# Attention scores as plain float32 products of two heads on the two halves of the array's rows

## The chip, the core and the metric

The kernel runs on one NeuronCore of a Trainium2 chip. Its engines work side by side and meet only at semaphores: TensorE (PE in the profile; its weight loads are PEld), VectorE (DVE), ScalarE (ACT), GpSimd (POOL) and SyncE (SP), which issues most of the DMAs. On-chip memory is SBUF; TensorE writes into PSUM. The metric is the device time of one execution in microseconds (us), lower is better. The times given are medians of several executions; the profile is one further execution with its own time.

## What is computed

One layer of an encoder: a windowed attention with grouped queries (256 tokens, 2048 features, 32 query heads, 8 key heads of 64 features, four query heads for each key head), then a squared-ReLU MLP, each with a modulation by a condition vector before it and a LayerNorm behind it. The change touches the attention between the rotary positions and the values:

```python
def windowed_gqa_sink(h, positions, w_qkv, b_qkv, sink, w_o, b_o):
    proj = h @ w_qkv + b_qkv
    q, k, v = jnp.split(proj, [...], axis=-1)
    q = q.reshape(B, S, ATTN_KV_HEADS, ATTN_GROUP, ATTN_HEAD_DIM)
    k = k.reshape(B, S, ATTN_KV_HEADS, ATTN_HEAD_DIM)
    ...
    q = apply_rope(q, ...); k = apply_rope(k, ...)
    ...
    s = jnp.einsum('bnqhgd,bnkhd->bnhgqk', qb, kw).astype(jnp.float32) * (ATTN_HEAD_DIM ** -0.5)
    s = jnp.where(valid[None, :, None, None], s, -jnp.inf)
    m = jnp.maximum(jnp.max(s, axis=-1, keepdims=True), sk)
    p = jnp.exp(s - m)
    p = p / (jnp.sum(p, axis=-1, keepdims=True) + jnp.exp(sk - m))
    o = jnp.einsum('bnhgqk,bnkhd->bnqhgd', p.astype(vw.dtype), vw)
    return o.reshape(B, S, ATTN_Q_HEADS * ATTN_HEAD_DIM) @ w_o + b_o
```

## The kernel before

All data is float32. The large products (query-key-value projection, output projection, both MLP layers) are made of three products in the float32r format: each operand is split into a high part in float32r and the rest, and `mm3` (L499 to L502) adds high by high, high by low and low by high into one PSUM bank. A weight arrives as 1 MB in a `raw` buffer (SP issues it at L204); ACT makes the high part `wh` (L249), DVE the low part `wl` (L220).

The attention is laid over the projections. After the queries, keys and first values are there, 21 slots run (L866): in a slot the weights of one projection step are multiplied in two parts of 12 matmuls each (L500 to L502, 128x512), first those of the last value columns (`qkv`, slots 0 to 4), then those of the output projection (`project`). Around and between the parts stand the pieces of the attention: `scores(n)` ahead of slot n, `normalise(n)` and `probs_T(n-1)` in its middle, `values(n-1)` behind every second slot, and the rotation and transposition of the next block of queries. n counts 16 units; a unit is four query heads for 128 query tokens. j is the block of eight query heads (two key heads), `t` the half of the tokens.

- `split_k` and `split_q` (L661 to L678): after the rotation (`rope`), ACT writes the float32r high part of keys or queries and DVE the low part. For queries the two parts of a head stand side by side (64 + 64 columns); for keys each part stands twice.
- `heads_T` (L680): TensorE transposes blocks of 128x128 (L687, in float32r, against `identr`), eight for a call, and ACT copies them out of PSUM (L689). A transposed block of queries has the 64 high features on the upper rows and the 64 low ones on the lower rows. Keys take four calls, each block of queries two.
- `scores(n)` (L705): for each of four heads of one key head, two float32r matmuls over all 128 rows, 256 keys wide (L718 with the keys' high part, L719 with their low part). DVE adds the mask and takes the minimum (L724), ACT the exponential (L733).
- `normalise` (L738): ACT scales the probabilities (L748).
- `probs_T` (L751): eight float32 transposes (L758), two ACT copies (L760).
- `values(n)` (L763): four float32 matmuls of 512 columns into 64 PSUM rows each, two on the lower and two on the upper half of the array's columns (L773); ACT and DVE split the result (L775, L776).

Two further pieces are in the same stage. The modulation rows (`Mod`) multiply streamed weights with the condition vector: `quad` (L309) puts four float32 matmuls on four strips of 32 array columns. Behind the last projection step stand the sums of the LayerNorm: `add_gated` (L781 to L783), `norm_scalars` (L787 to L797), `normed` (L812 on DVE, L810 on ACT), and then the transposes of the MLP's input (L936).

What order the instructions have on an engine is decided by the scheduler of the framework when the kernel is built; each engine then runs its own list in that order. So a change in one place can move others.

Of the kernel before, what the change touches and what calls it, by code (L numbers as in the profile page):

```python
# [11 lines left out]
F32 = mybir.dt.float32  # L12
# [7 lines left out]
D = 2048  # L20
# [28 lines left out]
def hybrid_kernel(ctx: ExitStack, tc: tile.TileContext, a, out: bass.AP):  # L49
# [39 lines left out]
    identr = cst.tile([128, 128], F32R, name="identr")  # L89
    nc.vector.tensor_copy(identr, ident)  # L90
# [570 lines left out]
    def split_k(A):  # L661
        hl = [[g4(F32R) for _ in range(2)] for _ in range(NT)]
        for t in range(NT):
            s = A[:, t * 512:t * 512 + 512].rearrange("p (h d) -> p h d", h=8)
            vh, vl = (z.rearrange("p (h e d) -> p h e d", h=8, e=2) for z in hl[t])
            for e in range(2):
                nc.scalar.copy(vh[:, :, e], s)
                nc.vector.tensor_sub(vl[:, :, e], s, f32(vh[:, :, e]))
        return hl

    def split_q(A):
        hl = [g4(F32R), g4(F32R)]
        for t in range(NT):
            v = hl[t].rearrange("p (h x d) -> p h x d", h=8, x=2)
            s = A[:, t * 512:t * 512 + 512].rearrange("p (h d) -> p h d", h=8)
            nc.scalar.copy(v[:, :, 0], s)
            nc.vector.tensor_sub(v[:, :, 1], s, f32(v[:, :, 0]))
        return hl  # L678

    def heads_T(src):  # L680

        out = g4(F32R)
        for pr in range(2):
            pt = pst.tile([128, 512], F32R, name="pt")
            for i in range(2):
                for t in range(NT):
                    nc.tensor.transpose(pt[:, i * 256 + t * 128:i * 256 + t * 128 + 128],  # L687
                                        src(t, pr * 2 + i), identr)
            nc.scalar.copy(out[:, pr * 512:pr * 512 + 512], f32(pt))  # L689
        return out  # L690

    kT = {}

    def k_heads(khl, half):
        for x in range(2):
            o = heads_T(lambda t, i: khl[t][x][:, (half * 4 + i) * 128:(half * 4 + i) * 128 + 128])
            for q in range(4):
                kT[x, half * 4 + q] = o[:, q * 256:q * 256 + 256]

    def q_heads(qhl, half):  # L700
        return heads_T(lambda t, i: qhl[t][:, (half * 4 + i) * 128:(half * 4 + i) * 128 + 128])

    qA, qhl, qT, PS, PP, PT, oT = {}, {}, {}, {}, {}, {}, {}

    def scores(n):  # L705

        j, s, t = n // 4, n % 2, n % 4 // 2
        g = 2 * j + s
        hs = slice(4 * g, 4 * g + 4)
        pss = []  # L710
        nm = sml.tile([128, 4], F32, name="nm")
        for rp in range(2):
            ps = psa.tile([128, 512], F32, name="pa")
            for i in range(2):
                r = 2 * rp + i
                o = ps[:, i * 256:i * 256 + 256]
                lq = qT[j, s][:, r * 256 + t * 128:r * 256 + t * 128 + 128]
                nc.tensor.matmul(o, lq, kT[0, g], start=True, stop=False)  # L718
                nc.tensor.matmul(o, lq, kT[1, g], start=False, stop=True)  # L719

            pv = ps.rearrange("p (i k) -> p i k", i=2)
            for i in range(2):
                h = 4 * g + 2 * rp + i
                nc.vector.tensor_tensor_reduce(out=pv[:, i], in0=pv[:, i], in1=msk[:, t], scale=-1.0,  # L724
                                               scalar=nsnk[:, h:h + 1], op0=OP.add, op1=OP.min,
                                               accum_out=nm[:, 2 * rp + i:2 * rp + i + 1])
            pss.append(pv)
# [476 lines left out]
```

## Time and profile before

| | us |
|---|---|
| median of three runs | 1105.11 (1102.15 to 1106.28) |
| profiled execution, its own time | 1102.22 |
| its span (first to last instruction) | 1100.4 |
| PE busy | 1071.0 |
| DVE busy | 810.7 |
| ACT busy | 535.0 |
| granted TensorE clock, mean | 0.995 of full speed |

The span has a loading stage (until about 156 us), the attention slots with the projections (156 to about 360 us), the first LayerNorm, and the MLP (from 369 us to the end). In the rows of the timeline the columns are: start in us, busy time in us, engine, line, operation, what it writes from what, array rows and columns and moving shape, and how many records were merged. Matmuls are pipelined, so a single one shows a longer time (0.28 or 0.39 us) than the distance between two starts (0.12 or 0.23 us); what a piece costs is read from starts. A plain float32 matmul leaves two records in the trace, a float32r one and a transpose leave one.

### The profile page before, as it was taken

How to read it: one execution, taken by the hardware profiler on the slowest of the kernel's cores; microseconds unless marked ns; L12 is line 12 of the kernel's file. 1: busy time of each engine (PE TensorE's matmuls, PEld its weight loads, DVE VectorE, ACT ScalarE, POOL GpSimd, SP SyncE). 2: the span in 40 equal slices, each digit the busy share in tenths (PEclk: the TensorE clock that was granted, in tenths of full speed). 3: DMA queues.
4: the chain of work that ended last, by engine and by line, in shares of the span. 5: the costliest groups of instructions: out<-in, count | busy, mean ns of one | idle time of the engine just before them, and what ended most of it. 6: DMA issues, size and time to landing. Idle time of an engine off the chain costs nothing.

```text
span 1100.4 us, 15640 instructions
## 1 busy us (share of the span) xinstructions
PE 1071.0 (97%) x6154; PEld 870.8 (79%) x6154; DVE 810.7 (74%) x1175; ACT 535.0 (49%) x832; POOL 30.0 (3%) x54
## 2 busy tenths in 40 slices
PE   8889999999999899999999999999999999999995
PEld 6667677767677799988888888888888888888884
DVE  5597899979899787764588889756666556665676
ACT  5332448876772736643345443344553334544340
POOL 1000000001000000000000010001000000000001
PEclk9999999999999999999999999999999999999998
DMA  9999986679985896555578778766555555557521
GB/s 384 425 426 426 426 364 258 245 279 377 416 325 205 345 357 255 192 191 191 191 279 310 278 290 334 304 231 211 186 189 191 197 198 187 178 187 267 192 76 76
DMA packets 43337, 292.70 MB, mean 266 GB/s; under 512 B 5104, under 2 KB 5232, under 8 KB 9472
## 3 DMA queue, kind: packets, MB, share of 16 engines
q1 hardware_dynamic: 39312, 279.85, 66.4%
q0 software_dynamic: 3200, 10.50, 2.8%
q10 hardware_dynamic: 752, 1.35, 0.3%
q8 instruction: 48, 0.79, 0.3%
q14 instruction: 25, 0.20, 0.0%
HBM read 289.57 MB, written 2.11 MB: 265 GB/s over the span
## 4 chain that ended last, share of the span: by engine, by line
PE 88%; DMA 6%; DVE 4%; ACT 1%; issue 1%; SPq 0%; DVEq 0%; ACTq 0%
PE pa L1030 16%; PE pa L500 16%; PE pa L502 16%; PE pa L501 16%; PE pa L1031 8%; DMA raw<-in_modm 3%; PE pa L1007 3%; PE pa L1006 3%; PE pa L1008 3%; PE pm L309 3%; DMA raw<-in_wqkv 3%; PE pa L773 2%; PE pt L758 1%; DVE wl L220 1%; PE pa L718 1%; PE pt L687 1%
## 5 line engine op out<-in xcount | busy, mean ns | idle before, releaser
L220 DVE TENSOR_TENSOR wl<-raw,wh 128x1024 fp32r<-128x1024 f32 x332 | 403.4, 1222 | 218.8 <-ACT wh L249 218.1
L249 ACT CAST wh<-raw 128x1024 fp32r<-128x1024 f32 x332 | 347.2, 1053 | 441.7 <-PE pa L502 221.8
L500 PE MATMUL pa<-wh,g 128*128 128x512 f32 x816 | 322.2, 396 | 6.4 <-ACT g L521 3.1
L502 PE MATMUL pa<-wh,g 128*128 128x512 f32 x816 | 318.1, 392 | 2.1 <-DVE g L523 2.1
L501 PE MATMUL pa<-wl,g 128*128 128x512 f32 x816 | 319.4, 391 | 0.0
L1030 PE MATMUL pa<-g,wh 128*128 128x512 f32 x768 | 270.1, 397 | 0.0
L1031 PE MATMUL pa<-g,wl 128*128 128x256 f32 x768 | 214.8, 280 | 0.0
L500 PEld LDWEIGHTS pa<-wh,g 128*128 128x128 f32 x816 | 153.4, 188 | 44.4 <-ACT g L521 4.2
L502 PEld LDWEIGHTS pa<-wh,g 128*128 128x128 f32 x816 | 153.1, 188 | 39.2 <-DVE g L523 5.3
L501 PEld LDWEIGHTS pa<-wl,g 128*128 128x128 f32 x816 | 153.5, 188 | 32.4 <-issue 1.7
L1030 PEld LDWEIGHTS pa<-g,wh 128*128 128x128 f32 x768 | 144.2, 188 | 36.0 <-issue 0.8
L1031 PEld LDWEIGHTS pa<-g,wl 128*128 128x128 f32 x768 | 144.8, 189 | 0.1
L347 DVE SCALAR_TENSOR_TENSOR g<-raw,cact,g 128x1024 f32<-128x1024 f32 x65 | 82.8, 1280 | 1.1 <-DMA raw<-in_modf 0.6
L1007 PE MATMUL pa<-g,wh 128*128 128x256 f32 x256 | 72.5, 284 | 0.6 <-DVE g L950 0.5
L1006 PE MATMUL pa<-g,wh 128*128 128x256 f32 x256 | 72.6, 286 | 0.3 <-ACT g L942 0.3
L1008 PE MATMUL pa<-g,wl 128*128 128x256 f32 x256 | 72.3, 283 | 0.0
L309 PE MATMUL pm<-raw,cact 128*32 128x256 f32 (+2 forms) x776 | 48.4, 370 | 3.3 <-DMA raw<-in_modm 3.0
L1006 PEld LDWEIGHTS pa<-g,wh 128*128 128x128 f32 x256 | 48.8, 192 | 1.4 <-issue 0.8
L1007 PEld LDWEIGHTS pa<-g,wh 128*128 128x128 f32 x256 | 49.0, 192 | 1.0 <-DVE g L950 1.0
L1008 PEld LDWEIGHTS pa<-g,wl 128*128 128x128 f32 x256 | 49.1, 192 | 0.0
L347 DVE SCALAR_TENSOR_TENSOR g4b<-raw,cact,g4b 128x1024 f32<-128x1024 f32 x32 | 40.7, 1280 | 10.8 <-DMA raw<-in_modgf 10.8
L309 PEld LDWEIGHTS pm<-raw,cact 128*32 128x32 f32 x776 | 20.7, 111 | 21.7 <-issue 8.7
(172 smaller groups left out, 806.8 us busy)
## 6 DMA issues: line engine op xcount, KB each, us to landing
raw<-in_w SPq DMA_DIRECT2D x64, 1024.0 KB, 4.8
raw<-in_w1b SPq DMA_DIRECT2D x48, 1024.0 KB, 4.9
raw<-in_modm SPq DMA_DIRECT2D x32, 1024.0 KB, 16.5
raw<-in_modf SPq DMA_DIRECT2D x32, 1024.0 KB, 7.2
raw<-in_wqkv SPq DMA_DIRECT2D x24, 1024.0 KB, 14.1
raw<-in_modgm SPq DMA_DIRECT2D x16, 1024.0 KB, 6.9
raw<-in_wo SPq DMA_DIRECT2D x16, 1024.0 KB, 8.4
raw<-in_w1a SPq DMA_DIRECT2D x16, 1024.0 KB, 7.2
```

The lines of the kernel that those rows point to most:

```text
L220: self.pinned(nc.vector.tensor_sub(l, r, f32(self.hs[n])))
L249: self.pinned(nc.scalar.copy(h, s))
L309: i = nc.tensor.matmul(self.ps[32 * j:32 * j + 32, :w], lhsT[j] if type(lhsT) is list else lhsT, rhs[j], start=self.first, stop=stop)
L347: nc.vector.scalar_tensor_tensor(p[:, :e], s, cact[:, kt:kt + 1], p[:, :e], op0=OP.mult, op1=OP.add)
L500: nc.tensor.matmul(ps, xh, wh, start=start, stop=False)
L501: nc.tensor.matmul(ps, xh, wl, start=False, stop=False)
L502: S.prev = nc.tensor.matmul(ps, xl, wh, start=False, stop=stop).ins
L1006: nc.tensor.matmul(o, wh(w, 128), hh, start=new, stop=False)
L1007: nc.tensor.matmul(o, wh(w, 128), hl, start=False, stop=False)
L1008: nc.tensor.matmul(o, wl(w, 128), hh, start=False, stop=end)
L1030: nc.tensor.matmul(ps, wh(k, 128), hb, start=k == 0, stop=False)
L1031: nc.tensor.matmul(ps[:, :256], wl(k, 128), hb[:, :256], start=False, stop=k == NK - 1)
```

## The change

Scores are made of float32 operands that are not split. `split_k`, `split_q` and the float32r identity go away. `pairs_T` transposes whole float32 blocks: one block of 128 columns holds a query (or key) head of each of the two key heads of a block j, so that after it the first key head's 64 features stand on the upper 64 rows and the second's on the lower. `scores(n)` then makes four float32 matmuls, each with 64 rows of the array: the heads of key head s = 0 on rows 0 to 63, those of s = 1 on rows 64 to 127, each half into a PSUM bank of its own. A unit n is now two heads of both key heads (`rh` tells which two) instead of four heads of one. `probs_T` writes its transposed probabilities into tiles shared by two units, so that `values` finds the four heads of a key head side by side. The query columns of the weights and the bias are put in the alternating order on the host.

```diff
-    def split_k(A):
...
-    def split_q(A):
-        hl = [g4(F32R), g4(F32R)]
-        for t in range(NT):
-            v = hl[t].rearrange("p (h x d) -> p h x d", h=8, x=2)
-            s = A[:, t * 512:t * 512 + 512].rearrange("p (h d) -> p h d", h=8)
-            nc.scalar.copy(v[:, :, 0], s)
-            nc.vector.tensor_sub(v[:, :, 1], s, f32(v[:, :, 0]))
-        return hl
-
-    def heads_T(src):
...
+    def pairs_T(src, n):
+
+        out = g4()
+        for pr in range(n // 2):
+            pt = pst.tile([128, 512], F32, name="pt")
             for i in range(2):
                 for t in range(NT):
-                    nc.tensor.transpose(pt[:, i * 256 + t * 128:i * 256 + t * 128 + 128],
-                                        src(t, pr * 2 + i), identr)
-            nc.scalar.copy(out[:, pr * 512:pr * 512 + 512], f32(pt))
+                    x = t * 512 + (pr * 2 + i) * 128
+                    nc.tensor.transpose(pt[:, i * 256 + t * 128:i * 256 + t * 128 + 128], src[:, x:x + 128], ident)
+            nc.scalar.copy(out[:, pr * 512:pr * 512 + 512], pt)
         return out
...
     def scores(n):
...
+        pss = [psa.tile([128, 512], F32, name="pa").rearrange("p (i k) -> p i k", i=2) for _ in range(2)]
         nm = sml.tile([128, 4], F32, name="nm")
-        for rp in range(2):
-            ps = psa.tile([128, 512], F32, name="pa")
+        for i in range(2):
+            x = (2 * rh + i) * 256 + t * 128
+            for s in range(2):
+                p = slice(64 * s, 64 * s + 64)
+                nc.tensor.matmul(pss[s][:, i], qT[j][p, x:x + 128], kT[p, j * 256:j * 256 + 256],
+                                 start=True, stop=True)
+        for s in range(2):
+
             for i in range(2):
-                r = 2 * rp + i
-                o = ps[:, i * 256:i * 256 + 256]
-                lq = qT[j, s][:, r * 256 + t * 128:r * 256 + t * 128 + 128]
-                nc.tensor.matmul(o, lq, kT[0, g], start=True, stop=False)
-                nc.tensor.matmul(o, lq, kT[1, g], start=False, stop=True)
...
     def probs_T(n):
...
-        pT = g4()
+        if n % 2 == 0:
+            PT[n // 2] = [g4() for _ in range(NT)]
...
-            nc.scalar.copy(pT[:, kt * 512:kt * 512 + 512], pt)
-        PT[n] = pT
+            nc.scalar.copy(PT[n // 2][kt].rearrange("p (s h x) -> p s h x", s=2, h=2)[:, :, n % 2],
+                           pt.rearrange("p (s x) -> p s x", s=2))
...
     kA = whole(rope(4, 0))
-    khl = split_k(kA)
     run(qkv(G - 1, 1))
-    qhl[0] = split_q(whole(rope(0, 1)))
+    qA[0] = whole(rope(0, 1))
     run(qkv(G - 1, 2))
-    k_heads(khl, 0)
-    run(qkv(*LATE[0]), [lambda: k_heads(khl, 1)])
-    for h in range(2):
-        qT[0, h] = q_heads(qhl[0], h)
+    kT = pairs_T(kA, 4)
+    run(qkv(*LATE[0]))
+    qT[0] = pairs_T(qA[0], 4)
...
-            if i == 2:
-                mid.append(lambda: qhl.__setitem__(j + 1, split_q(qA[j + 1])))
             if i == 3:
-                for h in range(2):
-                    mid.append(lambda h=h: qT.__setitem__((j + 1, h), q_heads(qhl[j + 1], h)))
+                mid.append(lambda: qT.__setitem__(j + 1, pairs_T(qA[j + 1], 4)))
```

The scheduler also orders the lists anew. In the changed file the lines have other numbers: L687 is the score matmul, L667 the transpose of queries and keys, L743 the value matmul, L728 the transpose of probabilities, L307 the modulation's matmul, L498 to L500 those of `mm3`, L218 the low part of a weight.

The first place is TensorE's list at the first `values`, in slot 3. Before, with L773 the value matmuls and L718 and L719 the scores of the next unit:

```order
L502 MATMUL pa<-wh,g_1261 128x512
L773 MATMUL pa<-g_1702,g_342 64x512
L718 MATMUL pa<-g_1463,g_1564 128x256
L773 MATMUL pa<-g_1786,g_342 64x512
L773 MATMUL pa<-g_1702,g_342 64x512
L773 MATMUL pa<-g_1786,g_342 64x512
L719 MATMUL pa<-g_1476,g_1564 128x256
L718 MATMUL pa<-g_1463,g_1564 128x256
```

In the changed kernel the same place, with L743 the values and L687 the scores, reads:

```order
L500 MATMUL pa<-wh,g_1259 128x512
L743 MATMUL pa<-g_1622,g_340 64x512 x2
L743 MATMUL pa<-g_1623,g_340 64x512 x2
L687 MATMUL pa<-g_1443,g_1492 128x256 x4
L498 MATMUL pa<-wh,g_1108 128x512
```

The four value matmuls now stand together, and the four score matmuls follow as one piece; before, a score matmul stood between the first value matmul and the other three.

The second place is TensorE's list at the scores of unit 2, which before stood as one piece of eight behind the modulation's four matmuls (the first two and the last two of the eight are shown):

```order
L758 MATMUL pt<-ident,g_1594 128x128 x2
L502 MATMUL pa<-wh,g_1111 128x512
L309 MATMUL pm<-raw,cact 32x512 x4
L718 MATMUL pa<-g_1463,g_1551 128x256
L719 MATMUL pa<-g_1476,g_1551 128x256
...
L718 MATMUL pa<-g_1463,g_1551 128x256
L719 MATMUL pa<-g_1476,g_1551 128x256
L500 MATMUL pa<-wh,g_1260 128x512
```

In the changed kernel, with L307 the modulation's matmuls:

```order
L500 MATMUL pa<-wh,g_1109 128x512
L687 MATMUL pa<-g_1443,g_1492 128x256
L307 MATMUL pm<-raw,cact 32x512 x4
L687 MATMUL pa<-g_1443,g_1492 128x256 x3
L498 MATMUL pa<-wh,g_1258 128x512
```

Here the modulation's matmuls moved into the score piece, which is cut in 1 and 3; it is the only one of the 16 that is cut.

The third place is DVE's list behind the last projection step, at the sums of the first LayerNorm (L781 to L783 are `add_gated`, L787 to L797 `norm_scalars`, L220 the low part of a weight of the MLP). Before:

```order
L783 BN_STATS st_3341<-g_2620 128x6
L220 TENSOR_TENSOR wl<-raw,wh 128x1024
L787 BN_AGGR mv<-st_3341 128x2
L781 TENSOR_TENSOR tmp<-pa,g4b 128x512
...
L386 TENSOR_SCALAR scf<-scf 128x4
L220 TENSOR_TENSOR wl<-raw,wh 128x1024
L793 RECIPROCAL r_3498<-sd 128x1
```

In the changed kernel (L751 to L753 are `add_gated`, L757 the first of `norm_scalars`):

```order
L218 TENSOR_TENSOR wl<-raw,wh 128x1024
L752 TENSOR_TENSOR g_2471<-g_2471,tmp 128x512
L751 TENSOR_TENSOR tmp<-pa,g4b 128x512
L753 BN_STATS st_3148<-g_2471 128x6
L752 TENSOR_TENSOR g_2471<-g_2471,tmp 128x512
L757 BN_AGGR mv<-st_3148 128x2
```

The two low parts moved ahead of the last two sums; none stands between them and the LayerNorm's scalars any more.

More of the change, by code (lines that the diff above doesn't have):

```diff
@@ L88, in hybrid_kernel @@
     make_identity(nc, ident)
-    identr = cst.tile([128, 128], F32R, name="identr")
-    nc.vector.tensor_copy(identr, ident)
     onesr = cst.tile([128, 128], F32R, name="onesr")
@@ L659, in whole @@
         return A
-    def split_k(A):
-        hl = [[g4(F32R) for _ in range(2)] for _ in range(NT)]
-        for t in range(NT):
-            s = A[:, t * 512:t * 512 + 512].rearrange("p (h d) -> p h d", h=8)
[L665 to L668, printed above, removed]
-        return hl
-    def split_q(A):
-        hl = [g4(F32R), g4(F32R)]
-        for t in range(NT):
-            v = hl[t].rearrange("p (h x d) -> p h x d", h=8, x=2)
-            s = A[:, t * 512:t * 512 + 512].rearrange("p (h d) -> p h d", h=8)
-            nc.scalar.copy(v[:, :, 0], s)
-            nc.vector.tensor_sub(v[:, :, 1], s, f32(v[:, :, 0]))
-        return hl
@@ L692, in hybrid_kernel @@
[L692 to L703, printed above, removed]
+                    x = t * 512 + (pr * 2 + i) * 128
@@ L705, in scores, with of @@
+                    nc.tensor.transpose(pt[:, i * 256 + t * 128:i * 256 + t * 128 + 128], src[:, x:x + 128], ident)
+            nc.scalar.copy(out[:, pr * 512:pr * 512 + 512], pt)
+        return out
+    qA, qT, PS, PP, PT, oT = {}, {}, {}, {}, {}, {}
     def scores(n):
[L707 to L710, printed above, removed]
+        j, rh, t = n // 4, n % 2, n % 4 // 2
+        def of(x):
+            return x.rearrange("p (g r i) -> p g r i", r=2, i=2)[:, 2 * j:2 * j + 2, rh]
+        pss = [psa.tile([128, 512], F32, name="pa").rearrange("p (i k) -> p i k", i=2) for _ in range(2)]
@@ L725, in scores @@
+        for s in range(2):
+            for i in range(2):
+                h = 4 * (2 * j + s) + 2 * rh + i
+                nc.vector.tensor_tensor_reduce(out=pss[s][:, i], in0=pss[s][:, i], in1=msk[:, t], scale=-1.0,
                                                scalar=nsnk[:, h:h + 1], op0=OP.add, op1=OP.min,
-                                               accum_out=nm[:, 2 * rp + i:2 * rp + i + 1])
-            pss.append(pv)
+                                               accum_out=nm[:, 2 * s + i:2 * s + i + 1])
@@ L728, in scores @@
         es = sml.tile([128, 4], F32, name="es")
-        nc.vector.tensor_add(es, nm, snk[:, hs])
+        nc.vector.tensor_tensor(es.rearrange("p (s i) -> p s i", s=2), nm.rearrange("p (s i) -> p s i", s=2),
+                                of(snk), op=OP.add)
         P = g4()
@@ L773, in values @@
                 nc.tensor.matmul(po[64 * s:64 * s + 64], acc[5][:, c:c + 64],
-                                 PT[n - 1 + s][:, kt * 512:kt * 512 + 512], start=kt == 0, stop=kt == 1)
+                                 PT[n // 2][kt][:, s * 512:s * 512 + 512], start=kt == 0, stop=kt == 1)
         nc.scalar.copy(oh, po)
@@ L1126, in _layout, with by_block @@
     cc = np.ascontiguousarray
+    def by_block(w):
+        w = np.array(w)
+        w[:, :D] = w[:, :D].reshape(-1, 4, 2, 4, DH).transpose(0, 1, 3, 2, 4).reshape(-1, D)
+        return w
     x = f(i["x"])[0]
```

11 lines of the change are left out of this document (2 added, 9 removed).

## The prediction

> **What bounds the kernel now.** I read the busy times of the page first, then the busy times by stretch, then what TensorE waits for in the stretch that the change touches.
>
> ```profile
> PE 1071.0 (97%) x6154; PEld 870.8 (79%) x6154; DVE 810.7 (74%) x1175; ACT 535.0 (49%) x832; POOL 30.0 (3%) x54
> ```
> ```profile
> 156.00:357.00 201.00, 200.13 (x1161) 143.30 (x1161) 184.88 (x358) 136.87 (x324) 8.27 (x14) 1.00 0.78 304
> ```
> ```profile
> PE pa L500 <- ACT g L733: 0.5, 1, 0.5
> PE pa L500 <- DVE g L539: 0.4, 1, 0.4
> ```
>
> The row of the stretch gives its length, then the busy time of PE, PEld, DVE, ACT and POOL with their instructions, the granted clock and the DMA engines' share. All of the change lies between 156 and 357 us. There PE is busy 200.1 of 201 us and waits 0.9 us in all; DVE has 16 us of idle time, ACT 64, and the DMA engines run at 0.78 of their time. So this stretch is as long as TensorE's list, and the change is worth what it takes from that list. A busy PE is a weak witness, since ends are modelled; so I priced TensorE's pieces by the starts around them. The matmuls of the projections start 0.23 us apart (more exactly 0.2275: 0.455 for two). A piece between them costs the time from the last start before it to the second start behind it, less 0.455 (the first start behind it still carries some of the change-over).
>
> ```profile
> 285.98 0.39 PE L501 MATMUL pa<-wl,g 128*128 128x512 f32 x1
> 286.21 0.80 PE L687 MATMUL pt<-identr,g 128*128 128x128 f32 x8
> ...
> 287.14 0.40 PE L500 MATMUL pa<-wh,g 128*128 128x512 f32 x1
> ```
> ```profile
> 303.08 0.39 PE L501 MATMUL pa<-wl,g 128*128 128x512 f32 x1
> 303.31 1.03 PE L758 MATMUL pt<-ident,g 128*128 128x128 f32 x8
> ...
> 304.41 0.39 PE L502 MATMUL pa<-wh,g 128*128 128x512 f32 x1
> ```
>
> **Transposes of queries and keys.** Eight in float32r cost 287.14 - 285.98 - 0.455 = 0.705 us; eight in float32 (those of the probabilities) 304.41 - 303.08 - 0.455 = 0.875. Before there are 12 such pieces (96 transposes), 8.5 us; the change leaves 40 float32 transposes, five pieces, 4.4 us. That is **-4.1 us**.
>
> **Scores.** A unit was eight float32r matmuls:
>
> ```profile
> 205.05 0.28 PE L718 MATMUL pa<-g,g 128*128 128x256 f32 x1
> ...
> 205.76 0.39 PE L500 MATMUL pa<-wh,g 128*128 128x512 f32 x1
> ```
>
> Six of the eight stand between these two rows' starts and take 205.76 - 205.05 = 0.71 us, so eight take 0.95. In their place come four float32 matmuls of 256 columns, two on each half of the rows. No run here shows halves of the rows; halves and quarters of the columns are there, in the modulation and the values:
>
> ```profile
> 282.93 0.39 PE L502 MATMUL pa<-wh,g 128*128 128x512 f32 x1
> 283.25 1.07 PE L309 MATMUL pm<-raw,cact 128*32 128x256 f32 x16
> ...
> 284.58 0.40 PE L501 MATMUL pa<-wl,g 128*128 128x512 f32 x1
> ```
> ```profile
> 333.95 0.39 PE L502 MATMUL pa<-wh,g 128*128 128x512 f32 x1
> 334.27 1.94 PE L773 MATMUL pa<-g,g 128*64 128x512 f32 x8
> ...
> 336.48 0.40 PE L501 MATMUL pa<-wl,g 128*128 128x512 f32 x1
> ```
> ```profile
> 192.38 0.39 PE L502 MATMUL pa<-wh,g 128*128 128x512 f32 x1
> 192.70 1.07 PE L773 MATMUL pa<-g,g 128*64 128x512 f32 x2
> 193.70 0.38 PE L718 MATMUL pa<-g,g 128*128 128x256 f32 x1
> 194.01 1.93 PE L773 MATMUL pa<-g,g 128*64 128x512 f32 x6
> 195.87 0.39 PE L719 MATMUL pa<-g,g 128*128 128x256 f32 x1
> 196.09 0.28 PE L718 MATMUL pa<-g,g 128*128 128x256 f32 x1
> ```
>
> One value matmul alone (two records, 512 columns) takes 193.70 - 192.70 = 1.00 us from start to the next start; the six records of the other three take 1.86, not 3. So the two halves run side by side, at about 0.43 us for a record of 512 columns and half of that for 256, and every change of the array's division costs something besides. The modulation's 16 records are four in a row on each strip, 256 columns each: 284.58 - 282.93 - 0.455 = 1.20 us. The new score piece is four in a row on each half, 256 columns each, so **1.20 us if the halves of the rows run side by side**. If they run one after the other it is eight in a row of 256, as long as the value piece with four in a row of 512: 336.48 - 333.95 - 0.455 = 2.07 us. I take 1.20, since that is what halves and quarters of the columns do in these rows, and keep 2.07 for the range.
>
> [...]
>
> Against a piece between projections on both sides, pieces with divided arrays that touch each other save a change-over:
>
> ```profile
> 255.70 0.39 PE L502 MATMUL pa<-wh,g 128*128 128x512 f32 x1
> 256.01 1.07 PE L309 MATMUL pm<-raw,cact 128*32 128x256 f32 x16
> 257.01 1.94 PE L773 MATMUL pa<-g,g 128*64 128x512 f32 x8
> ...
> 260.18 0.40 PE L501 MATMUL pa<-wl,g 128*128 128x512 f32 x1
> ```
>
> Behind the values follow the eight scores and one projection matmul. This costs 260.18 - 255.70 - 0.455 = 4.02; modulation, values and scores apart would be 1.20 + 2.07 + 0.95 = 4.22, so a joint saves 0.20. In the new order seven score pieces stand right behind values and two right behind the modulation: 9 x 0.20 = 1.8. The piece that is cut 1 and 3 by the modulation runs six in a row instead of four: +0.43. Scores: 16 x (1.20 - 0.95) - 1.8 + 0.4 = **+2.6 us**.
>
> **Cut pieces.** The old order cuts four value or modulation pieces, so that a half or some strips run alone. The first is above: from 192.38 to 196.09 are 3.71 us for values, two scores and a projection start, which together are 2.07 + 2 x 0.118 + 0.23 = 2.53; the cut costs 1.18. The others:
>
> ```profile
> 165.39 0.62 PE L500 MATMUL pa<-wh,g 128*128 128x512 f32 x2
> ...
> 169.94 0.40 PE L502 MATMUL pa<-wh,g 128*128 128x512 f32 x1
> ```
> ```profile
> 241.29 0.39 PE L500 MATMUL pa<-wh,g 128*128 128x512 f32 x1
> ...
> 244.68 0.39 PE L502 MATMUL pa<-wh,g 128*128 128x512 f32 x1
> ```
> ```profile
> 274.70 0.39 PE L502 MATMUL pa<-wh,g 128*128 128x512 f32 x1
> ...
> 280.62 0.40 PE L501 MATMUL pa<-wl,g 128*128 128x512 f32 x1
> ```
>
> At 165.39 (its second start is 0.23 later) 3.87 us are left over the 0.455, for two transposing pieces and one modulation piece, 2 x 0.705 + 1.20 = 2.61: 1.26 lost. At 241.29 2.94 for one of each, 1.90: 1.03 lost. At 274.70 5.46 for values, a modulation of half the length (1.20 - 0.43), scores and probabilities, 2.07 + 0.77 + 0.95 + 0.875 = 4.67: 0.79 lost. In the new order all values and modulation pieces are whole: **-4.3 us**. This part is the scheduler's, not the diff's.
>
> **Behind the projections.** PE waits for the LayerNorm there, which runs on DVE:
>
> ```profile
> 362.21 1.22 DVE L220 TENSOR_TENSOR wl<-raw,wh 128x1024 fp32r<-128x1024 f32 x1
> ...
> 364.25 0.55 DVE L812 TENSOR_SCALAR g<-g,mv,r 128x512 f32<-128x512 f32 x1
> ```
>
> This low part stands in the chain and moves ahead of the last sums. Full gain 1.2 us; but the first half's scalars now stand behind the second half's sums, a loss of about the same. I take **-0.5**, bounds -1.2 and +0.7.
>
> **What costs nothing.** DVE loses 12 low parts and ACT 12 high parts and 14 copies:
>
> ```profile
> L677 DVE TENSOR_TENSOR g<-g,g 128x512 fp32r<-128x512 f32 x8 | 5.2, 681 | 0.2
> L668 DVE TENSOR_TENSOR g<-g,g 128x512 fp32r<-128x512 f32 x4 | 2.5, 686 | 0.0
> L689 ACT CAST g<-pt 128x512 fp32r<-128x512 f32 x24 | 13.1, 590 | 6.0 <-PE pt L687 5.9
> ```
>
> These 7.7 us of DVE lay beside PE's list and are worth nothing while PE is late; they keep DVE out of the way when PE's list gets shorter (177 us in a stretch of 195, 91%, after 92%). The probabilities' copies write pieces of 256 columns now; if that were slower, ACT's 64 idle us cover it. The first scores stand one projection matmul behind their queries' transposes, whose copy takes 0.59: a wait between 0 and 1.2 us; I take nothing, as some old transposes wait for such copies too. The lists of SP and POOL are the same as before.
>
> **Sum.** -4.1 + 2.6 - 4.3 - 0.5 = -6.3 us. From the profiled execution's 1102.2 that gives 1095.9, from the median of 1105.1 it gives 1098.8. The profiled run is as fast as the fastest of the three, so I forecast **1098**, nearer the median; own range 1094 to 1102.
>
> **Rivals.**
> 1. *The halves of the rows take turns* (the change does not do what it says). Then the score pieces cost 16 x (2.07 - 0.95) - 1.8 = 16.1 instead of 2.6, and the sum is +7.2: 1109.4 to 1112.3, **1111**, slower. The place is the 16 score pieces. It decides from 6.3 / 16 = 0.4 us on: a piece of 1.6 us or more eats the whole gain. For it: nothing here shows divided rows, and both halves write all 128 PSUM rows. Against: divided columns do run side by side, also in float32, and the two halves have banks of their own. Chance 0.12.
> 2. *Weight loads come out from under the matmuls.* Loads of 0.19 us before each of four passes would add 16 x 4 x 0.19 = 12 us: +5.9, **1110**. Against it stands the old score piece: each matmul has its own load, and they start 0.118 us apart.
>
> ```profile
> L719 PEld LDWEIGHTS pa<-g,g 128*128 128x128 f32 x64 | 12.1, 189 | 1.4 <-issue 1.2
> ```
>
> [...] Chance 0.04.
> 3. *The gain turns into waits.* PE, ahead by 6 us, waits for DVE's minima, for ACT or for a weight. For it: DVE is busy 92% here, and the new order is tight at the first scores. Against: 0.9 us of waits before, and DVE gets lighter. It gives 1102 to 1105, **1104**. Chance 0.10.
>
> **How the numbers follow.** The forecast has 0.74. A change of over 0.5% (5.5 us) is about what a measurement of this kernel can tell from none; the forecast lies just beyond it, so of its 0.74 I give 0.46 to faster and 0.28 to the same. Rival 3 is the same (0.10); rivals 1 and 2 are slower but for 0.02. Faster 0.46, same 0.40, slower 0.14. Of the forecast's own range and rival 3 some 0.78 is held up to 1105; the bound of the unknown price asks for more, so the range is 1094 to 1111.
>
> **What would show it.** In the changed profile: the score pieces' records in pairs a few ns apart, and about 1.20 us for a piece between projections (2.07 would be rival 1, about 2 with even gaps rival 2); five transposing pieces of 0.88; no value piece split; PE's waits between 156 and 352 us still about 1 us; the stretch from the first transposes to the last projection matmul shorter by 5.8; ahead of it and in the MLP nothing moved. Waits on DVE or ACT of several us would show rival 3. The forecast is wrong if a score piece is over 1.6 us, or if the MLP's length changes.

## The result, and the profile after

The changed kernel takes **1095.85 us** (median of five runs, 1095.11 to 1100.0) against 1103.55 for the kernel before on the same chip: the ratio is 0.9932 with a 95% interval of 0.9917 to 0.9948, 7.7 us less. A second series of the same program gave 1095.35 and 0.9924 (0.9907 to 0.9940). The forecast was 1098, range 1094 to 1111, with "faster by over 0.5%" the likeliest sign.

The profiled execution after is the slowest of its five (1100.0 us, span 1098.2), so it is read beside that of the second series, "again" (span 1093.8). First the busy times of the page after:

```profile
PE 1067.6 (97%) x6098; PEld 863.1 (79%) x6098; DVE 804.2 (73%) x1162; ACT 522.0 (48%) x806; POOL 30.0 (3%) x54
```

TensorE has 56 records and 3.4 us less, VectorE 6.5 us, ScalarE 13 us. The view by stretches of the kernel after (length, then busy time of PE, PEld, DVE, ACT and POOL, granted clock, DMA share, GB/s), for a piece of the loading stage and for the stretch from the first transposes to the last projection matmul:

```profile
75.00:100.00 25.00, 24.55 (x117) 18.23 (x118) 21.43 (x28) 8.08 (x10) 0.00 (x0) 0.86 1.01 425
...
159.50:357.95 198.45, 195.07 (x1113) 135.18 (x1111) 180.14 (x349) 129.28 (x305) 8.22 (x14) 1.00 0.79 304
```

The same view of "again":

```profile
157.97:353.51 195.54, 194.87 (x1112) 135.22 (x1111) 179.87 (x349) 129.18 (x305) 8.22 (x14) 1.00 0.79 309
```

Cut at the same marks, the kernel before has 202.57 us there (156.52 to 359.09). The profiled execution after entered the stretch 3 us late: the clock granted to TensorE was 0.86 from 75 to 100 us, where the change touches nothing. Other profiles bear this out, all with 1.00 from 100 to 150 us: with 1.00 from 75 to 100 us as well, the stretch begins at 156.52 us (before) and 156.70 (`spread_1`), with 0.93 there at 157.97 ("again") and 158.00 (the run with the parts put back), with 0.86 at 159.50 (this one, where the clock was half from 75.00 to 81.83 us). So those 3 us of its 1100.0 are no effect of the change. What TensorE waits for between 150 and 368 us (total, times, longest), after:

```profile
PE pm L307 <- DMA raw<-in_modf: 3.2, 2, 2.1
PE pa L500 <- DVE g L746: 1.1, 1, 1.1
PE pa L972 <- DVE g L915: 0.4, 1, 0.4
PE pt L667 <- ACT g L730: 0.2, 1, 0.2
```

and "again":

```profile
PE pm L307 <- DMA raw<-in_modf: 1.6, 2, 1.1
PE pa L972 <- DVE g L915: 0.4, 1, 0.4
PE pt L667 <- ACT g L730: 0.2, 1, 0.2
```

`in_modf` are the modulation's weights (L307 multiplies them on TensorE, L345 on VectorE), L746 the low part of the values. Up to the last projection matmul the waits are 3.3 us in the first profile and 0.6 in "again", against 0.9 before; behind it they are 1.5 us in both, against 3.0 before. So the changed list need not wait longer than the old one. The 2.7 us between the two executions are nearly the 2.9 us between the two stretches.

The stages of each kernel, from the starts of the first transposes, the last projection matmul and the first MLP matmul with a low part of the input (L1007 before, L972 after), in us; the two parts of the MLP are 186.0 and 544.8 in every kernel:

| kernel | first transposes at | slots with projections | LayerNorm |
|---|---|---|---|
| before | 156.52 | 202.57 | 10.54 |
| after | 159.50 | 198.45 | 9.49 |
| again | 157.97 | 195.54 | 9.48 |

From before to "again" the two stages lose 7.03 + 1.06 = 8.1 us; the timed medians of that series differ by 8.3 (1103.67 to 1095.35).

The score piece of the changed kernel, in the timeline (start, duration, what it is; x counts records, two for a float32 matmul):

```profile
174.95 0.39 PE L500 MATMUL pa<-wh,g 128*128 128x512 f32 x1
175.27 1.13 PE L687 MATMUL pa<-g,g 64*128 64x256 f32 x8
176.34 0.50 PE L498 MATMUL pa<-wh,g 128*128 128x512 f32 x1
176.67 0.40 PE L499 MATMUL pa<-wl,g 128*128 128x512 f32 x1
```

It costs 176.67 - 174.95 - 0.455 = 1.265 us. The eight records stand in pairs: 175.272 and 175.279, 175.592 and .599, 175.808 and .815, 176.024 and .030.

### The profile page after: what moved, and what is told of

The parts are those of the page before. It is cut to its first block, busy times and chain, and to the rows that moved or that the text cites. A ratio compares the mean times of both kernels' runs of the same rounds, so it can differ in the third digit from the quotient of the medians.

```text
span 1098.2 us, 15487 instructions
## 1 busy us (share of the span) xinstructions
PE 1067.6 (97%) x6098; PEld 863.1 (79%) x6098; DVE 804.2 (73%) x1162; ACT 522.0 (48%) x806; POOL 30.0 (3%) x54
## 4 chain that ended last, share of the span: by engine, by line
PE 86%; DVE 7%; DMA 4%; ACT 2%; issue 1%; DVEq 0%; ACTq 0%
PE pa L995 16%; PE pa L500 15%; PE pa L498 15%; PE pa L499 15%; PE pa L996 8%; PE pa L972 3%; PE pa L971 3%; PE pa L973 3%; PE pm L307 3%; DVE wl L218 2%; DMA raw<-in_modm 2%; DMA raw<-in_modf 1%; DVE g L345 1%; DMA raw<-in_wqkv 1%; PE pa L687 1%; PE pa L743 1%
## 5 line engine op out<-in xcount | busy, mean ns | idle before, releaser
L218 DVE TENSOR_TENSOR wl<-raw,wh 128x1024 fp32r<-128x1024 f32 x332 | 403.9, 1223 | 223.6 <-ACT wh L247 222.9
L247 ACT CAST wh<-raw 128x1024 fp32r<-128x1024 f32 x332 | 347.1, 1051 | 441.3 <-PE pa L500 228.6
L498 PE MATMUL pa<-wh,g 128*128 128x512 f32 x816 | 324.1, 398 | 5.1 <-ACT g L519 2.6
L500 PE MATMUL pa<-wh,g 128*128 128x512 f32 x816 | 318.9, 392 | 4.1 <-DVE g L521 3.0
L498 PEld LDWEIGHTS pa<-wh,g 128*128 128x128 f32 x816 | 153.9, 189 | 46.8 <-issue 7.5
L500 PEld LDWEIGHTS pa<-wh,g 128*128 128x128 f32 x816 | 153.5, 188 | 41.2 <-DVE g L521 6.0
L345 DVE SCALAR_TENSOR_TENSOR g<-raw,cact,g 128x1024 f32<-128x1024 f32 x65 | 82.6, 1280 | 2.8 <-DMA raw<-in_modf 2.3
L972 PE MATMUL pa<-g,wh 128*128 128x256 f32 x256 | 72.7, 285 | 0.4 <-DVE g L915 0.4
L307 PE MATMUL pm<-raw,cact 128*32 128x256 f32 (+2 forms) x776 | 48.8, 375 | 5.9 <-DMA raw<-in_modf 3.2
L972 PEld LDWEIGHTS pa<-g,wh 128*128 128x128 f32 x256 | 49.1, 192 | 0.9 <-DVE g L915 0.8
L345 DVE SCALAR_TENSOR_TENSOR g4b<-raw,cact,g4b 128x1024 f32<-128x1024 f32 x32 | 40.7, 1280 | 9.0 <-DMA raw<-in_modgf 8.8
L307 PEld LDWEIGHTS pm<-raw,cact 128*32 128x32 f32 x776 | 20.9, 112 | 25.9 <-issue 11.5
## 6 DMA issues: line engine op xcount, KB each, us to landing
raw<-in_wqkv SPq DMA_DIRECT2D x24, 1024.0 KB, 12.8
```

The costliest lines, as they stand in the source:

```text
L218: self.pinned(nc.vector.tensor_sub(l, r, f32(self.hs[n])))
L247: self.pinned(nc.scalar.copy(h, s))
L307: i = nc.tensor.matmul(self.ps[32 * j:32 * j + 32, :w], lhsT[j] if type(lhsT) is list else lhsT, rhs[j], start=self.first, stop=stop)
L345: nc.vector.scalar_tensor_tensor(p[:, :e], s, cact[:, kt:kt + 1], p[:, :e], op0=OP.mult, op1=OP.add)
L498: nc.tensor.matmul(ps, xh, wh, start=start, stop=False)
L500: S.prev = nc.tensor.matmul(ps, xl, wh, start=False, stop=stop).ins
```

## The experiments

Every ratio is to the kernel before, timed beside it; each of these series has five rounds.

### The same kernel again

> The changed kernel once more, for a second profile and for times beside the other three runs. The first profile of it showed two things that the forecast did not have: a clock of 0.86 between 75 and 100 us, ahead of the change, and 3.2 us in which TensorE waits for weights of the modulation (in_modf) with 1.1 us for DVE between 255 and 265 us. If the waits belong to the new order, they come again at about the same size and the stretch from the first transposes to the last projection matmul is again 198 to 199 us; if they came from the low clock ahead of it, they are gone and the stretch is 195 to 196 us. Time 1096 us either way.

Measured: 1095.35 us, ratio 0.9924 (0.9907 to 0.9940). The stretch is 195.54, and the waits in it are 0.6 us instead of 3.3, with the same list. So the long waits of the first profile are a matter of the execution; what made the weight late there is not shown.

### Both key heads on the same half of the rows

```diff
             for s in range(2):
-                p = slice(64 * s, 64 * s + 64)
+                p = slice(0, 64)
```

The scores of the second key head are made from the first one's queries and keys; TensorE gets as many matmuls of the same size, all on rows 0 to 63.

> Both key heads' score matmuls read rows 0 to 63 (the second key head's scores are then those of the first: that part of the computation is replaced), so that the two products can't lie side by side; banks, counts and everything behind them stay. Theory 1 (the two halves of the rows run side by side, and this makes the 1.26 us of a score piece): a piece becomes 2.07 us or somewhat more, 16 x 0.81 = 13 us, 1109 us. Theory 2 (a matmul over 64 rows is cheap by itself, wherever it lies): no change, 1096 us.

Measured: 1107.27 us, ratio 1.0030 (1.0018 to 1.0041). The timeline of this kernel:

```profile
172.60 0.39 PE L500 MATMUL pa<-wh,g 128*128 128x512 f32 x1
172.92 1.99 PE L687 MATMUL pa<-g,g 64*128 64x256 f32 x8
174.84 0.50 PE L498 MATMUL pa<-wh,g 128*128 128x512 f32 x1
175.18 0.40 PE L499 MATMUL pa<-wl,g 128*128 128x512 f32 x1
```

A piece costs 175.18 - 172.60 - 0.455 = 2.125 us, and its records start one by one: the second 320 ns behind the first, the others 216 ns apart (172.916, 173.236, 173.451 and on). TensorE's busy time in the scores, by line, of this kernel:

```profile
L687 PE MATMUL pa<-g,g 64*128 64x256 f32 x128 | 32.1, 390 | 0.0
```

and of the changed kernel:

```profile
L687 PE MATMUL pa<-g,g 64*128 64x256 f32 x128 | 19.3, 403 | 0.0
```

The same 128 records cover 32.1 or 19.3 us. The halves working side by side are worth 16 x (2.125 - 1.265) = 13.8 us by the pieces; the timed difference is 11.9 (1107.27 - 1095.35). By starts the 16 pieces differ by 12.8, since the first one and the cut one grow by 0.4 only, and transposes and modulation pieces that are held up in "again" cost 1.4 less here. Without the halves side by side the change loses.

### The halves in another order in the list

```diff
-        for i in range(2):
-            x = (2 * rh + i) * 256 + t * 128
-            for s in range(2):
+        for s in range(2):
+            for i in range(2):
+                x = (2 * rh + i) * 256 + t * 128
```

> The four score matmuls of a unit in another order: both of the first half, then both of the second, instead of alternating. If each half takes its next matmul as soon as it is free, whatever stands between in the list: the piece stays at 1.26 us and the time at 1096 us. If matmuls start in the order of the list and only neighbours on different halves overlap: the piece runs six passes of 256 columns in a row instead of four, +0.43 us for each of 16, 6.9 us, 1103 us.

Measured: 1099.54 us, ratio 0.9956 (0.9939 to 0.9974), between the two. The timeline and TensorE's waits tell them apart:

```profile
172.08 0.39 PE L500 MATMUL pa<-wh,g 128*128 128x512 f32 x1
172.40 1.14 PE L687 MATMUL pa<-g,g 64*128 64x256 f32 x8
...
173.81 0.40 PE L499 MATMUL pa<-wl,g 128*128 128x512 f32 x1
```
```profile
260.29 1.07 PE L307 MATMUL pm<-raw,cact 128*32 128x256 f32 x16 [2.58 <-DMA raw<-in_modf]
```

The piece costs 173.81 - 172.08 - 0.455 = 1.275, as before the swap, and its records still stand in pairs, 13 ns apart instead of 7. So a half does not wait for the other half's matmuls ahead of it in the list. The slots are 5.2 us longer all the same (200.78 instead of 195.54), and 3.1 of that lie in one other place: at 260.29 a modulation piece stands ahead of the eight transposes of probabilities that it cut in the changed kernel, and waits 2.58 us for a weight ("again": 0.46). By starts the two pieces cost 5.61 us there instead of 2.56. Not all of that is the wait, for behind it the clock was half:

```profile
261.45:264.86 3.41, 3.41 (x13) 3.03 (x13) 1.63 (x4) 2.26 (x5) 0.00 (x0) 0.50 1.02 430
```

In this stretch transposes start 213 ns apart instead of 109 and projection matmuls 427 instead of 227, some 1.5 us in all, of which about 0.6 fall behind the two pieces. This is the mechanism of the third rival (the gain turns into waits). How much of the wait belongs to the new list and how much to the one execution, a single profile does not tell.

### The old kernel with whole pieces

Order-only links keep value, modulation, score and transposing pieces of the kernel before together:

```diff
+        def link(self, i):
+            if self.chain:
+                if self.tail is not None:
+                    tc.add_manual_dep(i.ins, self.tail.name, ORDER_ONLY, reason="whole")
+                self.tail = i.ins
+            return i
...
-                nc.tensor.matmul(o, lq, kT[0, g], start=True, stop=False)
+                S.link(nc.tensor.matmul(o, lq, kT[0, g], start=True, stop=False))
```

> The kernel before, with order-only edges that keep its value, modulation, score and query-transpose pieces in the order of the program, so that three of its four cut pieces are whole (one modulation piece is still cut in two by a projection matmul). Theory 1 (cut pieces cost what the starts around them show): 1.18 + 0.79 + 1.26 = 3.2 us less than before, 1100 us. Theory 2 (the gain of the change comes from DVE and ACT work that is gone): no change against before, 1103.5 us.

Measured: 1101.05 us, ratio 0.9973 (0.9961 to 0.9986); the slots take 201.05 us, the LayerNorm 9.47. TensorE's waits:

```profile
PE pm L317 <- DVE g L356: 1.8, 2, 1.1
PE pm L317 <- DMA raw<-in_modf: 1.1, 1, 1.1
PE pa L510 <- DVE wl L228: 0.9, 1, 0.9
```

So a part of the gain is the order alone and could be had without the change: 3.0 us by the ratio. Three of the four cut pieces are whole in this build (one modulation piece is still cut by a projection matmul); they cost 3.2 of the 4.3 us. The slots keep 1.5 of these; the waits in the slots rise from 0.9 to 2.6 us, all of them for VectorE (L356 and L228, the modulation's sums and a weight's low part in this file), which still carries the low parts of keys and queries here. The 1.1 us for `in_modf` and the shorter LayerNorm are as in the changed kernel, so the LayerNorm's part of the gain can be had by order alone, too.

### The removed high and low parts put back

All 12 ScalarE copies and 12 VectorE subtractions of `split_k` and `split_q` are put into the changed kernel where they stood; nothing reads their results.

```diff
     kA = whole(rope(4, 0))
+    split_k(kA)
     run(qkv(G - 1, 1))
     qA[0] = whole(rope(0, 1))
+    split_q(qA[0])
...
+            if i == 2:
+                mid.append(lambda: split_q(qA[j + 1]))
```

> The changed kernel with the 12 low parts (DVE) and 12 high parts (ACT) of keys and queries put back, their results unused; the float32 transposes and scores stay. The order changes a little with them (one modulation piece is cut 1 and 3 by a score piece, about +0.9 us). Theory 1 (that work lay beside TensorE's list): score and transpose pieces as in the changed kernel, stretch of the attention 196 to 198 us, time 1096 to 1097 us. Theory 2 (the gain came from DVE and ACT being relieved): most of the gain is gone, 1101 us or more.

Measured: 1104.12 us, ratio 1.0005 (0.9991 to 1.0019): the whole gain is gone. But not all of this is the work put back, as the traces show. The stretch of the opening, from the first transposes to the first ones of probabilities, by the view of stretches; "again" has the same 102 TensorE records there:

```profile
158.00:177.70 19.70, 19.70 (x102) 14.70 (x101) 19.25 (x39) 12.53 (x25) 0.00 (x0) 1.00 0.92 361
```

and with the parts put back:

```profile
158.00:183.30 25.30, 22.85 (x102) 16.57 (x101) 24.63 (x45) 14.04 (x29) 0.00 (x0) 0.93 0.84 332
```

The timeline of TensorE there, with the parts put back (L684 the transposes, L704 the scores, L719 the exponential):

```profile
167.51 1.03 PE L684 MATMUL pt<-ident,g 128*128 128x128 f32 x8
...
174.22 1.13 PE L704 MATMUL pa<-g,g 64*128 64x256 f32 x4
177.80 1.16 PE L704 MATMUL pa<-g,g 64*128 64x256 f32 x4 [2.45 <-ACT g L719]
```

5.6 of the 8.0 us that the slots lose (203.51 instead of 195.54) lie in the opening. VectorE is busy 24.63 of 25.30 us there; the keys and first queries reach TensorE later (the second transposes at 167.51 instead of 164.31), and the second score piece stops in its middle, for 2.45 us, for the first one's exponential. This is the order of ScalarE's list:

```profile
174.37 1.04 ACT L247 CAST wh<-raw 128x1024 fp32r<-128x1024 f32 x1 [3.87 <-issue]
175.44 1.28 ACT L719 ACT_TABLE_LOAD   x1
176.73 0.47 ACT L719 ACTIVATE g<-pa,nm 128x256 f32<-128x256 f32 x1
```

The high part of a weight (L247) stands ahead of the first exponential here, and behind the first four in "again". It waits until 174.31 for a projection matmul (L500), while the minimum that the exponential needs has been there since 172.96. Behind the stop the granted clock is half, and projection matmuls start 427 ns apart instead of 227, 1.5 us more by starts:

```profile
178.76:182.17 3.41, 3.41 (x9) 2.60 (x9) 3.38 (x10) 2.44 (x8) 0.00 (x0) 0.50 0.63 262
```

So two things are mixed in this run: the work put back, and an order that moved with it. The stop and the half clock make about 4 of the 5.6 us, and a modulation piece that is cut again about 0.9.

### The low parts taken out of the old kernel

```diff
-        hl = [[g4(F32R) for _ in range(2)] for _ in range(NT)]
+        hl = [[g4(F32R)] * 2 for _ in range(NT)]
...
-                nc.vector.tensor_sub(vl[:, :, e], s, f32(vh[:, :, e]))
...
-            nc.scalar.copy(v[:, :, 0], s)
-            nc.vector.tensor_sub(v[:, :, 1], s, f32(v[:, :, 0]))
+            nc.scalar.copy(v, s[:, :, None, :].to_broadcast([128, 8, 2, 64]))
```

> The kernel before without VectorE's 12 low parts of keys and queries: the keys' low operand is the high one, the queries' low part a copy of the high one, written by one wider ScalarE copy. So the low parts are left out of the scores; TensorE has the same matmuls and transposes as the kernel before, and pieces cut much as there. Theory 1 (TensorE's list sets the length, and VectorE's relief is worth something only when that list is shorter too): 1101 to 1103.5, at most 2.5 us below the kernel before. Theory 2 (VectorE's relief in the opening is the gain, whatever TensorE's list is): 1098 or less.

Measured: 1103.6 us, ratio 1.0012 (1.0003 to 1.0021). The opening of the kernel before:

```profile
156.50:182.50 26.00, 25.13 (x142) 19.31 (x141) 24.87 (x45) 18.23 (x37) 0.00 (x0) 1.00 0.82 323
```

and without the low parts:

```profile
156.80:182.40 25.60, 24.80 (x142) 19.04 (x141) 21.26 (x40) 18.78 (x36) 0.00 (x0) 1.00 0.77 306
```

VectorE has 3.6 us less to do there and the stretch is 0.4 us shorter; all slots together take 202.46 us, against 202.57. So VectorE's relief alone is worth nothing in the old list. What it is worth once TensorE's list is cut, the run before this one does not tell by itself, since the larger part of its loss in the opening is order; the next three divide it.

### Only the later parts, only VectorE's, only ScalarE's

Three runs divide the work that was put back: the later three blocks of queries (both engines), and of the opening VectorE's six subtractions or ScalarE's six copies alone.

```diff
+            if i == 2:
+                mid.append(lambda: split(qA[j + 1], 1))
```

> The changed kernel plus the high and low parts of the three later blocks of queries (six ScalarE copies, six VectorE subtractions, results unused), not those of the opening. Theory 1 (the loss with all twelve lies in the opening, 156 to 183 us, where VectorE is full): 1096 or less, the opening still near 19.7 us. Theory 2 (each low part costs about the same anywhere): half of the 8.8 us that the twelve cost, about 1100.

Measured: 1098.18 us, ratio 0.9955 (0.9942 to 0.9968). The opening is untouched (19.70 us), as the first theory had it, and still 2.9 us are lost, nearly all behind 230 us: the sums of a modulation there come late from VectorE, and TensorE waits for modulation weights.

```profile
PE pm L307 <- DMA raw<-in_modf: 2.3, 2, 1.3
PE pa L983 <- DVE g L926: 0.4, 1, 0.4
PE pa L500 <- DVE g L755: 0.3, 1, 0.3
PE pm L307 <- DVE g L345: 0.2, 1, 0.2
```

The other two put `split(kA, 2)` and `split(qA[0], 1)` behind the two `whole` calls of the opening, with one of the two operations each.

> The changed kernel plus only the six VectorE subtractions of the opening (keys and first queries; 4 us of VectorE, results unused), no ScalarE copies. Theory 1 (a full VectorE in the opening holds TensorE up): 1100 or more, with the opening (first transposes to first probability transposes) at 23 us or more instead of 19.7. About 0.9 of that is the list: one modulation piece is cut in this build. Theory 2 (the loss came from ScalarE's copies or from the order): at most 1097.

Measured: 1099.21 us, ratio 0.9961 (0.9947 to 0.9975). The opening:

```profile
158.10:179.60 21.50, 20.33 (x102) 14.47 (x101) 21.50 (x38) 11.74 (x22) 0.00 (x0) 1.00 0.88 338
```

VectorE is busy without a gap, and TensorE waits 1.17 us for an earlier transposing piece to be copied out. But the stretch grew by 1.8 us only, not by 3.3, and 0.9 of that is the cut piece; the stop of the run with all twelve and its half clock are not there. The rest of the loss is again behind 230 us, where a modulation piece among transposes of probabilities costs 3.8 instead of 2.6.

> The changed kernel plus only the six ScalarE copies of the opening (4 us, results unused), no VectorE subtractions. Theory 1 (VectorE is what is full): 1095 to 1097. Theory 2 (ScalarE's copies delay the first scores): 1100 or more.

Measured: 1096.34 us, ratio 0.9939 (0.9925 to 0.9953); the opening takes 19.43 us. ScalarE's copies alone hold nothing up.

By the ratios the twelve parts cost 8.9 us (1.0005 - 0.9924 of 1103.6), and their thirds 3.4 (later), 4.1 (VectorE's in the opening) and 1.7 (ScalarE's in the opening, whose interval meets that of "again"): 9.2 in all, as near as these intervals allow. Both theories were too simple. In the traces the loss sits where TensorE waits or a piece is cut, in the opening and at the modulation near 230 to 265 us. VectorE's and ScalarE's parts of the opening lengthen it by 5.6 us together, and by 1.8 and -0.3 alone; the stop for the exponential and the half clock behind it, about 4 us, which only the first build has, are as much as the difference. The order of the list differs in all these builds, and no run puts the work back in the order of the changed kernel. So how much the work itself costs, and how much the order that comes with it, stays open.

### The modulation's weights spread over other slots

`SLOT_FILL` says in how many steps the modulation's weights are planned into each slot; slot 11 has 5. Three variants of the changed kernel, the added lines from first to third:

```diff
-    SLOT_FILL = dict(enumerate([0, 1, 2, 1, 0, 1, 3, 0, 1, 3, 2, 0, 3, 5, 1, 1, 3, 2, 1, 3, 0, 0, 1], -2))
+    SLOT_FILL = dict(enumerate([0, 1, 2, 1, 0, 1, 3, 0, 1, 3, 2, 0, 3, 3, 2, 2, 3, 2, 1, 3, 0, 0, 1], -2))
+    SLOT_FILL = dict(enumerate([0, 1, 2, 1, 0, 1, 3, 0, 1, 3, 2, 1, 3, 3, 2, 1, 3, 2, 1, 3, 0, 0, 1], -2))
+    SLOT_FILL = dict(enumerate([0, 1, 2, 1, 0, 1, 3, 1, 1, 2, 2, 2, 2, 3, 2, 2, 2, 2, 2, 2, 0, 0, 1], -2))
```

> The changed kernel with the plan of the modulation's weights spread: of five steps between two output projection weights two go one and two places later. Its profiles show 1.6 to 3.8 us of waits for these weights. If the waits come from the burst of five, they fall under 1 us and the time to 1094 us. If they come from the DMA queue as a whole being behind at that place, they only move: 1095 to 1096 us.

> The same with one of the five a place later and one two places earlier. Burst theory: waits under 1 us, 1094 us. Queue as a whole: the waits stay or grow, since one load more stands ahead of the tight place: 1096 to 1097 us.

> The modulation's weights spread evenly, one or two (once three) in every place of the plan from the sixth on. Burst theory: no waits within the slots, 1094 us. Queue as a whole: 1095 to 1097 us.

Measured: 1094.27 us (ratio 0.9916, 0.9901 to 0.9931), 1095.04 (0.9918, 0.9903 to 0.9933) and 1100.58 (0.9961, 0.9946 to 0.9977). TensorE's waits of the first:

```profile
PE pm L307 <- DMA raw<-in_modf: 1.2, 1, 1.2
PE pa L972 <- DVE g L915: 0.4, 1, 0.4
PE pt L667 <- ACT g L730: 0.2, 1, 0.2
```

and of the third:

```profile
PE pa L500 <- DVE g L746: 2.1, 1, 2.1
PE pm L307 <- DVE g L345: 1.2, 1, 1.2
PE pm L307 <- DMA raw<-in_modf: 1.1, 1, 1.1
```

Without the burst the wait for weights in the slots is gone (the 1.2 us left lie in the LayerNorm). `spread_1` is faster than the kernel before and has the lowest median of all, but its interval overlaps that of the unchanged plan, so that it beats the changed kernel is not shown. Spreading evenly was a miss: 3.3 us of waits for VectorE (the values' low part at L746, the modulation's sums at L345) take the place of the burst.

## Why the prediction was right, point by point

The sums below are for "again" against the profile of before, both by starts.

| step | predicted | measured |
|---|---|---|
| transposes of queries and keys | -4.1 | -3.4 |
| first scores wait | 0 (0 to 1.2) | +0.6 |
| scores | +2.6 | +3.5 |
| cut pieces | -4.3 | -4.3 (as worked out) |
| behind the projections | -0.5 (-1.2 to +0.7) | -1.06 |
| not in the sum (the rest) | | -3.4 |
| sum | -6.3 | -8.1 |

- **Bound.** The slots are as long as TensorE's list, as read: TensorE is busy 194.87 of 195.54 us after the change. The runs add that in the opening VectorE is nearly as busy (24.87 of 26.00 us before), and that neither step alone gives much in the old kernel (nothing without the low parts, 1.5 us in the slots with whole pieces).
- **Transposes.** Five pieces, as said, of 0.88, 0.80, 0.94, 1.32 and 1.16: 5.1 us instead of 4.4, as the later ones stand close behind other transposes: the last two begin only when ScalarE has copied those out (0.04 us behind the copies' ends, at 237.60 and 280.18). The first scores cost 0.63 us more than the others:

```profile
165.58 1.60 PE L687 MATMUL pa<-g,g 64*128 64x256 f32 x8
```

  Only 0.16 of that is the wait for the copy of their queries that the prediction had bounded and taken at nothing. The other 0.47 is a wait that it did not have: the second half of the rows begins at 166.05, 0.05 us behind the end of a sum of VectorE (L537, to 166.00) that reads a projection out of the same PSUM buffers (`pa`).
- **Scores.** The mechanism was right and the size off: a piece costs 1.265 instead of 1.20, and the cut one 2.88 together with its modulation. The joints hold: scores behind values cost 1.06, so 0.20 is saved. In sum 18.8 us after 15.3.
- **Rival 1** (the halves take turns) is refuted: pairs 7 ns apart, and 2.125 us a piece on one half, near the 2.07 that it was priced at.
- **Rival 2** (weight loads come out from under the matmuls) is refuted too. The loads of the piece on one half (line, engine, then count, busy time and mean ns):

```profile
L687 PEld LDWEIGHTS pa<-g,g 64*128 64x128 f32 x128 | 22.6, 186 | 12.5 <-issue 8.8 <-ACT g L702 0.4 <-ACT g L717 0.4
```

  They take 186 ns each on the same rows as the running pass, and passes still start 216 ns apart.
- **Cut pieces.** None of the four old cuts recurs, so the term stands as it was worked out. That the price is the order's and not the diff's is borne out by the old kernel with whole pieces, though there only 1.5 of 3.2 us stay.
- **Behind the projections.** This gave twice what was taken, near the bound, but not by the step that the prediction named:

```profile
356.52 0.69 DVE L753 BATCH_NORM_STATS2 st<-g 128x6 f32<-128x512 f32 x1
...
357.24 0.26 DVE L757 BATCH_NORM_AGGREGATE mv<-st 128x2 f32<-128x24 f32 x1
...
358.79 0.54 DVE L782 TENSOR_SCALAR g<-g,mv,r 128x512 f32<-128x512 f32 x1
```

  In "again" no low part stands between the sums, the scalars and the normalisation any more, and still the first normalisation begins no earlier: 5.28 us behind the start of the last projection matmul (358.79 - 353.51), against 5.16 before (364.25 - 359.09). The second half's sums and scalars, now ahead of it, take the time that the low part gave up. What comes earlier is ScalarE's share of the normalisation, which waits for a scalar (`nmr`) that VectorE now makes behind its first piece and made behind its fourth. Before:

```profile
366.52 1.52 ACT L810 ACTIVATE g<-g,nmr,r 128x512 f32<-128x512 f32 x2 [2.42 <-DVE nmr L807]
```

  and in "again":

```profile
359.43 1.52 ACT L780 ACTIVATE g<-g,nmr,r 128x512 f32<-128x512 f32 x2 [1.50 <-DVE nmr L777]
```

  These are 7.43 and 5.92 us behind the last projection matmul, and the transposes of this share begin 1.06 us earlier (360.75 - 353.51 after, 367.39 - 359.09 before). So the first half of the prediction's sum there, a gain and a loss of about the same, held; that ScalarE gains was not in it.
- **Not in the sum.** The old list lost 3.4 us that I had not priced. It is the difference that the other rows leave. Its largest parts are the two waits of TensorE that the view gave with 0.9 us: by starts they cost 1.3 (0.68 behind 178.06, and a score piece of 1.57 instead of 0.96 at 175.33), they stood in the opening, and both are gone. I had read them as a proof that nothing waits, not as something to win. The other 2 us are spread over some eight places, pieces in fragments among projections that lost 0.1 to 0.6 each; none was measured apart.
- **What costs nothing.** "Worth nothing while PE is late; they keep DVE out of the way when PE's list gets shorter": the first half holds, by the run without low parts (1.0012). The second fits the runs with parts put back (1.0005 with all, 0.9939 to 0.9961 with a third each), but order moved in each of them, so it is not shown apart. And I averaged VectorE over the whole stretch (92%); in the opening it was busy 24.87 of 26.00 us.
- **Rival 3** (the gain turns into waits) came in one of the two executions: 3.3 us of waits in the slots in the first profile, 0.6 in "again", against 0.9 before. The runs with the halves in another order and with the even spread show what it costs when they grow.
- **Luck.** Three terms came out worse than predicted, by 2.2 us together (transposes, first scores, scores); the 3.4 us that were not priced and 0.6 behind the projections more than made up for it. The bound and the halves working side by side were right; that the total lies within 2 us of the sum is in part luck.

## What to carry to other kernels

Price a divided array's pieces from starts, with the change-over in it, and refute or confirm "side by side" by putting both halves' work on one half. When one engine's list is to be cut, look at the busy time of the next engine stage by stage, not over the whole span: where both are nearly full, as in the opening here, a gain on one can be lost on the other. Rebuild after any edit and read the new order of every engine's list: here a build with two loops exchanged was 4 us slower through a wait elsewhere, and in the build with the parts put back one weight ahead of an exponential cost TensorE more than any other single place. Count waits by the same stages before and after, and look at the clock granted behind the longest ones: here some 1.5 us of slow clock stood behind a wait of 2.45 us and one of 2.58.

## What the runs showed of the hardware

- Two halves of the rows work side by side in plain float32 as well: in the changed kernel matmuls of 64 rows and 256 columns, two passes each, start in pairs 7 ns apart, and a pass follows on its half after 216 ns (the second of a piece after 320); a piece costs 1.265 us, with both products on one half 2.125.
- A half takes its next matmul past those of the other half in the list: with the halves in the other order, two matmuls of one half stand ahead, and the pairs are 13 ns apart; a piece costs 1.275 us.
- Weight loads on the rows in use take 186 ns each (mean, both products on one half), and the passes behind the second start 216 ns apart.
- TensorE's granted clock was half for 3.41 us behind a wait of 2.45 us (parts put back) and behind one of 2.58 us (halves in another order); behind the longest of the changed kernel's first profile, 2.07 us, it was 1.00. At half clock projection matmuls started 427 ns apart instead of 227, some 1.5 us for the stretch.
- Half clock comes in the loading stage too, and differs between executions of one program: from 75 to 100 us the changed kernel was granted 0.86 in the first profile (half for 6.83 us at a time) and 0.93 in "again", and its slots begin at 159.50 and 157.97 us. In one execution that is a good part of the effect sought, so stages are compared, not totals.
